# Sums for the activations' operands, and the third norm's factor and bias, moved from GpSimd to VectorE

## Chip, cores and metric

The kernel runs on one core of a Trainium2 chip. The metric is device time in microseconds (us), the median of three runs. The engines are TensorE (PE in the rows; PEld is its weight load), VectorE (DVE), ScalarE (ACT), GpSimd (POOL) and SyncE (SP), which issues the DMAs. Each works off its own queue in order.

## Reference

One decoder block, batch 1, 1024 tokens, width 1024, in float32: a SwiGLU layer (inner width 2816), a token mixer (short convolution beside a diagonal state space), a second SwiGLU layer and a gated embedding, each followed by a layer norm. Cut to what matters here:

```python
def layer_norm(x, g, b):
    xc = x - mean(x)
    return xc * rsqrt(mean(xc * xc) + LN_EPS) * g + b

x = layer_norm(ALPHA * x + 0.5 * swiglu(x, ffn1_w_in, ffn1_w_out), ln1_g, ln1_b)
mix = token_mixer(x, mix_w_in, ...)
x = layer_norm(ALPHA * x + mix, ln2_g, ln2_b)
x = layer_norm(ALPHA * x + 0.5 * swiglu(x, ffn2_w_in, ffn2_w_out), ln3_g, ln3_b)
e = (p @ ple_w_in) * sigmoid(x @ ple_w_gate)
x = layer_norm(ALPHA * x + e, ln4_g, ln4_b)
```

## The kernel before

**Products.** Every float32 operand is split into a rounded high part and a remainder (`split`, lines 175 and 176: ScalarE casts the high part, VectorE, or GpSimd where the code says so, subtracts it to get the low part), and a product is three passes of matmuls: high by high, high by low, low by high. Weights come as tiles `Ws` of 128x512 and are split into `Wh` and `Wl`.

**Seven products in place of eight.** The input layers (`w_in` of both SwiGLU layers and of the mixer) multiply 2x2 blocks by a Strassen-Winograd scheme. A pair of weight rows (`Pair`) needs seven operands of the activations: 11 and 21 are blocks as they are, 22 also, and t1, t2, t3 and t4 are sums of blocks: t1 = 12 - 11, t2 = 22 - t1, t3 = 22 - 12, t4 = 21 - t2. The same sums of weights (`Pair.rest`, lines 79, 84, 88, 96 and 102) run on GpSimd, and the change does not touch them.

**Where the activations' sums are made.** In three places. At the kernel's start `first_operands.later` (lines 426 to 437) makes them from `x` in two column groups j of 128x1024: j = 0 on VectorE, j = 1 on GpSimd. After the first and after the second layer norm `winograd_sink` (lines 365 to 373) gets two token tiles at a time, transposed by TensorE (line 281) and given factor and bias by ScalarE (line 283, `features`). For token pairs i = 2 and 3 it makes the four sums for each j: j = 0 on GpSimd, j = 1 on VectorE. Low parts of 11 and 21 (`x11l`, `x21l`) are mostly on GpSimd and stay there. While this goes on, TensorE works on the products by 11 and 21 of the first five pairs (`EARLY`, tiles `early`) and then needs t1, t2, t3, 22 and t4.

**The last stage** (from line 1229). For each of eight token tiles s: `apply(acc2[s])` gives factor and bias of the third layer norm to the residual stream (`affine`, lines 315 and 316: first half of the columns on VectorE, second half on GpSimd, each a multiply and an add of 128x512). Then, for each half of the columns, 24 matmuls make the gate into a `pm` bank (line 1243; there are six) and 6 matmuls the embedding into a `pt` bank (line 1248; there are two). ScalarE makes `sg`, the sigmoid (line 1251, a buffer of tag `T`; there are six, and the four rows `gb` of factor and bias are of that tag too), VectorE multiplies embedding and sigmoid (line 1252, which frees both banks' data) and adds the product to the residual stream (line 1253). The fourth layer norm follows (`moments`, lines 248 to 255, and lines 1257 and 1258), and a DMA writes the result.

**The order** of each engine's queue is set at build time by a scheduler that goes by dependences and its own estimate of times. `issue_after` adds an edge that keeps what is traced inside it, on the same engine, behind a given instruction.

Of the kernel before, what the change touches and what calls it, by code (L numbers as in the profile page):

```python
# [12 lines left out]
ALU = mybir.AluOpType  # L13
# [92 lines left out]
class Block:  # L106
# [194 lines left out]
    def affine(self, g, b, tag):  # L301

        if tag == "A8":
            both = self.t("A8", [P, 2, D], name="gb")
            gb = [both[:, v, 512 * h:512 * h + 512] for v in range(2) for h in range(2)]
        else:
            gb = [self.t(tag, [P, 512], name="gb") for _ in range(4)]
        for i, part in enumerate(gb):
            self.nc.sync.dma_start(part, (g, b)[i // 2][i % 2 * 512:i % 2 * 512 + 512].partition_broadcast(P))

        def apply(t):
            for h in range(2):
                sl = slice(h * 512, (h + 1) * 512)
                eng = (self.nc.vector, self.nc.gpsimd)[h]
                eng.tensor_tensor(t[:, sl], t[:, sl], gb[h], ALU.mult)
                eng.tensor_tensor(t[:, sl], t[:, sl], gb[2 + h], ALU.add)  # L316
        return apply


# [20 lines left out]
    def winograd_sink(self, xs, gb):  # L340

        kept = []
        gps = self.nc.gpsimd

        def put(name, y, i, j, eng=None):
            cols, ks = slice((i % 2) * 256, (i % 2 + 1) * 256), slice(2 * j, 2 * j + 2)
            hi, lo = xs[name]
            self.split(y, hi[:, ks, cols], lo[:, ks, cols], eng)

        def sink(i, pair):  # L350
            if i < 2:
                kept.append([self.t("H", [P, 4, 256], name="y") for _ in range(2)])
                for kh in range(2):
                    for j in range(2):
                        y = kept[i][kh][:, 2 * j:2 * j + 2]
                        self.features(pair, gb, 4 * kh + 2 * j, y)
                        put(("11", "21")[kh], y, i, j, None if (kh, j) == (0, 1) else gps)
                return
            for j in range(2):
                b11, b21 = (kept[i - 2][kh][:, 2 * j:2 * j + 2] for kh in range(2))  # L360
                b12, b22 = self.t("T", [P, 2, 256], name="b12"), self.t("T", [P, 2, 256], name="b22")
                t1 = self.t("T", [P, 2, 256], name="t1")
                self.features(pair, gb, 2 * j, b12)
                eng = (gps, self.nc.vector)[j]
                eng.tensor_tensor(t1, b12, b11, ALU.subtract)
                put("t1", t1, i, j)
                self.features(pair, gb, 4 + 2 * j, b22)
                put("22", b22, i, j)
                eng.tensor_tensor(b12, b22, b12, ALU.subtract)
                put("t3", b12, i, j)  # L370
                eng.tensor_tensor(t1, b22, t1, ALU.subtract)
                put("t2", t1, i, j)
                eng.tensor_tensor(t1, b21, t1, ALU.subtract)
                put("t4", t1, i, j)
        return sink
# [4 lines left out]
    def first_operands(self, xT, w_in):  # L380

        nc = self.nc
        xs = self.new_xs()
        self.open_region("init")
        p, w = {}, {}
        early = FIRST[:EARLY]

        def weight(f, kh):
            w[f, kh] = self.stage(w_in[f][kh])

        def piece(n, j):
            kh, th = int(n[0]) - 1, int(n[1]) - 1
            p[n, j] = self.r("xp", [P, 2, 512], 8)
            return xT[:, kh, th, 2 * j:2 * j + 2, :]

        def put(n, j, y, ks=slice(0, 2)):
            hi, lo = xs[n]
            k0 = slice(2 * j + ks.start, 2 * j + ks.stop)
            self.split(y[:, ks], hi[:, k0], lo[:, k0])

        weight(early[0], 0)
        for j in range(2):
            src = piece("11", j)
            for k in range(2):
                ks = slice(k, k + 1)
                nc.sync.dma_start(p["11", j][:, ks], src[:, ks])
                put("11", j, p["11", j], ks)
            weight(early[1 + j], 0)
        for f in early[3:]:
            weight(f, 0)  # L410
        for j in range(2):
            src = piece("21", j)
            nc.sync.dma_start(p["21", j], src)
            put("21", j, p["21", j])
        for n in ("12", "22"):
            for f in (early[:2] if n == "12" else early[2:]):
                weight(f, 1)
            for j in range(2):
                src = piece(n, j)
                nc.sync.dma_start(p[n, j], src)  # L420

        def later():
            tt = [self.t("H", [P, 2, 512], name="t1") for _ in range(2)]
            eng = (nc.vector, nc.gpsimd)
            for j in range(2):
                eng[j].tensor_tensor(tt[j], p["12", j], p["11", j], ALU.subtract)
                put("t1", j, tt[j])
            for j in range(2):
                eng[j].tensor_tensor(tt[j], p["22", j], tt[j], ALU.subtract)
                put("t2", j, tt[j])  # L430
            for j in range(2):
                eng[j].tensor_tensor(p["12", j], p["22", j], p["12", j], ALU.subtract)
                put("t3", j, p["12", j])
            for j in range(2):
                put("22", j, p["22", j])
            for j in range(2):
                eng[j].tensor_tensor(tt[j], p["21", j], tt[j], ALU.subtract)
                put("t4", j, tt[j])
        return xs, w, later

# [708 lines left out]
    def run(self, a, out):  # L1149
        nc = self.nc  # L1150
# [41 lines left out]
        acc2, last = self.mixer(state["x"], a, acc)  # L1192
# [19 lines left out]
        apply = self.affine(a["ln3_g"], a["ln3_b"], "T")  # L1212
# [11 lines left out]
        for v in ("ln4_g", "ln4_b"):  # L1224
            for h in range(2):
                tl = self.t("Ws", [P, 512], name="gb4")
                nc.sync.dma_start(tl, a[v][h * 512:(h + 1) * 512].partition_broadcast(P))
                gb4.append(tl)
        for s in range(NT):
            cols = slice((s % 4) * P, (s % 4 + 1) * P)  # L1230
            if s % 2 == 0:
                pp = self.split_w(self.stage(a["pT"][:, s // 2]))
            apply(acc2[s])
            pcol = lambda k: slice((2 * (s % 2) + k) * P, (2 * (s % 2) + k + 1) * P)
            cuts = HALVES if s < NT - 1 else (slice(0, 512), slice(512, 768), slice(768, D))
            for sl in cuts:
                dh, n = sl.start // 512, sl.stop - sl.start
                col = slice(sl.start - 512 * dh, sl.stop - 512 * dh)
                pg = self.pm()[:, :n]
                for k in range(NK):  # L1240
                    xx = self.op(xb[k // 4][s // 4])
                    for i, (p, q) in enumerate(((0, 0), (0, 1), (1, 0))):
                        nc.tensor.matmul(pg, xx[p](k % 4)[:, cols], wg[dh][k][q][:, col],  # L1243
                                         start=(k == 0 and i == 0), stop=(k == NK - 1 and i == 2))
                pe = self.pt()[:, :n]
                for k in range(2):
                    for i, (p, q) in enumerate(((0, 0), (0, 1), (1, 0))):
                        nc.tensor.matmul(pe, pp[p][:, pcol(k)], wp[q][:, k, sl], start=(k == 0 and i == 0),  # L1248
                                         stop=(k == 1 and i == 2))
                sg = self.t("T", [P, 512], name="sg")[:, :n]  # L1250
                nc.scalar.activation(sg, pg, AF.Sigmoid)
                nc.vector.tensor_tensor(sg, pe, sg, ALU.mult)
                nc.vector.scalar_tensor_tensor(acc2[s][:, sl], sg, 1.0 / ALPHA, acc2[s][:, sl], ALU.mult, ALU.add)
            mean, y, _ = self.moments(acc2[s], cuts)
            for dh, sl in enumerate(HALVES):
                t = acc2[s][:, sl]
                nc.vector.scalar_tensor_tensor(t, t, mean, gb4[dh], ALU.subtract, ALU.mult)
                nc.vector.scalar_tensor_tensor(t, t, y, gb4[2 + dh], ALU.mult, ALU.add)
                nc.sync.dma_start(out[:, s, sl], t)
# [62 lines left out]
```

## Time and profile before

| what | value |
|---|---|
| median of three runs | 2084.79 us (2083.38 to 2086.32) |
| the profiled execution's own time | 2086.58 us |
| its span, first to last instruction | 2084.8 us |
| mean granted TensorE clock | 0.991 |
| busy: PE, DVE, ACT, POOL | 96%, 80%, 39%, 41% of the span |

The profile is one execution. A row of its timeline says when an instruction (or a run of equal ones, xN) started, how long it took, and in brackets how long its engine had been idle before it and what ended that. The clock is in shares of 2.4 GHz: 1.00 is 2.4 GHz, 0.50 is 1.2 GHz.

### The profile page before, as it was taken

What the parts mean: (1) busy time and instruction counts of PE and PEld (TensorE: products, weight loads), DVE (VectorE), ACT (ScalarE), POOL (GpSimd) and SP (SyncE); (2) the same over time, 40 slices, a digit from 0 to 9 for tenths busy, and PEclk for the clock granted to TensorE, in tenths of its full rate; (3) what the DMA queues carried; (4) which work ended last, traced back from release to release, by engine and by line L of the source; (5) the groups of instructions that cost most, each with busy time, mean ns of one, the idle gap of its engine ahead of it and who ended that gap; (6) DMA issues with size and microseconds to landing.
All of it is one profiled execution on the core that took longest, in us unless ns stands there. A gap on an engine that the chain in (4) does not pass through costs nothing.

```text
span 2084.8 us, 26465 instructions
## 1 busy us (share of the span) xinstructions
PE 2001.7 (96%) x9030; PEld 1633.4 (78%) x9030; DVE 1668.0 (80%) x2560; ACT 813.7 (39%) x1422; POOL 846.4 (41%) x562
## 2 busy tenths in 40 slices
PE   7999999999999899999999999999999999999988
PEld 5887778776788777887878888788888876788867
DVE  7789888879998976767644679877667789998897
ACT  5333343445342545343533415533333345342520
POOL 3644444454313454333201372654444444313360
PEclk9999999999999999999999999999999999999999
DMA  4433343556540264333382410243323246431111
GB/s 170 127 117 96 122 141 126 179 186 223 164 141 25 106 187 148 100 122 114 133 299 80 151 53 17 83 149 117 101 87 126 91 166 217 162 128 69 54 45 69
DMA packets 153238, 260.24 MB, mean 125 GB/s; under 512 B 16144, under 2 KB 61200, under 8 KB 153104
## 3 DMA queue, kind: packets, MB, share of 16 engines
q1 hardware_dynamic: 153104, 258.56, 37.6%
q8 instruction: 71, 1.16, 0.2%
q14 instruction: 63, 0.52, 0.1%
HBM read 189.85 MB, written 68.65 MB: 124 GB/s over the span
## 4 chain that ended last, share of the span: by engine, by line
PE 67%; DVE 21%; issue 5%; DMA 2%; ACT 2%; POOL 2%; SPq 0%; DVEq 0%; POOLq 0%; ACTq 0%
PE pm L198 42%; PE pm L615 11%; PE pm L209 5%; PE pm L229 5%; DVE Wl L176 4%; PE pm L1243 2%; DVE wt L176 2%; DVE w L176 1%; DVE acc L622 1%; DVE ln L254 1%; PE pt L1248 1%; DVE ln L248 1%; DVE ln L255 1%; DVE acc L316 1%; DVE acc L234 1%
## 5 line engine op out<-in xcount | busy, mean ns | idle before, releaser
L175 ACT CAST Wh<-Ws 128x512 fp32r<-128x512 f32 x268 | 166.6, 622 | 346.5 <-PE pm L198 277.5
L176 DVE TENSOR_TENSOR Wl<-Ws,Wh 128x512 fp32r<-128x512 f32 x268 | 212.8, 799 | 109.1 <-ACT Wh L175 108.7
L175 ACT CAST Wh<-s 128x512 fp32r<-128x512 f32 x240 | 149.2, 622 | 379.2 <-PE pm L198 139.3
L176 DVE TENSOR_TENSOR Wl<-s,Wh 128x512 fp32r<-128x512 f32 x240 | 213.5, 890 | 25.8 <-ACT Wh L175 25.7
L615 PE MATMUL pm<-wt,Wh 128*128 128x512 f32 x640 | 188.0, 392 | 2.5 <-DVE acc L622 2.5
L84 POOL TENSOR_TENSOR s<-s,Ws 128x512 f32<-128x512 f32 x60 | 90.2, 1503 | 203.6 <-DVE Wl L176 193.3
L102 POOL TENSOR_TENSOR u<-u,p 128x512 f32<-128x512 f32 x60 | 96.1, 1602 | 144.3 <-DVE u L92 93.2
L615 PE MATMUL pm<-w,Wh 128*128 128x512 f32 x480 | 141.4, 392 | 6.1 <-ACT Wh L175 5.5
L622 DVE SCALAR_TENSOR_TENSOR acc<-pm,acc 128x512 f32<-128x512 f32 x200 | 132.7, 682 | 15.5 <-PE pm L615 14.8
L615 PEld LDWEIGHTS pm<-wt,Wh 128*128 128x128 f32 x640 | 119.7, 188 | 30.2 <-DVE acc L622 3.3
L79 POOL TENSOR_TENSOR s<-Ws 128x512 f32<-128x512 f32 x60 | 82.5, 1374 | 133.8 <-DVE Wl L176 102.0
L96 POOL TENSOR_TENSOR s<-Ws,s 128x512 f32<-128x512 f32 x60 | 92.3, 1538 | 108.8 <-DVE Wl L176 107.4
L615 PE MATMUL pm<-wt,Wl 128*128 128x512 f32 x320 | 113.8, 394 | 3.9 <-DVE Wl L176 3.6
L615 PEld LDWEIGHTS pm<-w,Wh 128*128 128x128 f32 x480 | 90.0, 189 | 26.8 <-ACT Wh L175 7.1
L198 PE MATMUL pm<-x11h,Wh 128*128 128x512 f32 (+1 forms) x264 | 99.1, 384 | 5.0 <-ACT x11h L175 5.0
L198 PE MATMUL pm<-x11h,Wl 128*128 128x512 f32 (+1 forms) x264 | 99.3, 379 | 3.1 <-DVE Wl L176 3.1
L198 PE MATMUL pm<-x11l,Wh 128*128 128x512 f32 (+1 forms) x264 | 99.6, 380 | 1.9 <-DVE x11l L176 1.3
L198 PE MATMUL pm<-xt1h,Wl 128*128 128x512 f32 x240 | 95.3, 397 | 5.3 <-DVE Wl L176 5.3
L198 PE MATMUL pm<-x21h,Wl 128*128 128x512 f32 x240 | 95.1, 396 | 5.5 <-DVE Wl L176 5.5
L198 PE MATMUL pm<-xt2h,Wl 128*128 128x512 f32 x240 | 94.8, 395 | 4.2 <-DVE Wl L176 4.1
L198 PE MATMUL pm<-xt4h,Wl 128*128 128x512 f32 x240 | 94.1, 392 | 4.6 <-DVE Wl L176 4.6
L198 PE MATMUL pm<-xt1l,Wh 128*128 128x512 f32 x240 | 94.4, 393 | 2.1 <-DVE xt1l L176 2.1
(355 smaller groups left out, 5615.7 us busy)
## 6 DMA issues: line engine op xcount, KB each, us to landing
Ws<-in_ffn_w_in SPq DMA_DIRECT2D x196, 256.0 KB, 2.7
Ws<-in_ffn_w_out SPq DMA_DIRECT2D x88, 256.0 KB, 3.1
Ws<-in_w_mix SPq DMA_DIRECT2D x74, 256.0 KB, 2.7
s<-h_s SPq DMA_DIRECT2D x60, 256.0 KB, 3.0
h<-a SPq DMA_DIRECT2D x58, 256.0 KB, 2.3
ha<-h SPq DMA_DIRECT2D x20, 512.0 KB, 4.1
hb<-h SPq DMA_DIRECT2D x20, 512.0 KB, 4.6
h_s<-u SPq DMA_DIRECT2D x20, 256.0 KB, 2.6
```

Source lines behind the costliest of these rows:

```text
L79: gps.tensor_tensor(s, a21, a22, ALU.add)
L84: gps.tensor_tensor(s, s, a11, ALU.subtract)
L96: gps.tensor_tensor(s, a12, s, ALU.subtract)
L102: gps.tensor_tensor(u3, u3, p5, ALU.add)
L175: self.nc.scalar.copy(hi, src)
L176: (lo_eng or self.nc.vector).tensor_tensor(lo, src, hi.bitcast(F32), ALU.subtract)
L198: self.nc.tensor.matmul(ps[:, tok], w[a][:, sl], x[b](k)[:, tok], start=(start and k == 0 and i == 0), stop=(k == nk - 1 and i == 2), skip ...
L209: self.nc.tensor.matmul(ps[h], w[a][:, sl], x(h)[b](k), start=(k == 0 and i == 0), stop=(k == 3 and i == 2))
L229: nc.tensor.matmul(ps, a[:, s * P:(s + 1) * P], b[:, cols], start=(j == 0 and i == 0), stop=(j == n - 1 and i == 2))
L615: nc.tensor.matmul(ps[i], hh[p][:, cols], w[n][:, j, q], start=(start and j == 0 and k == 0), stop=(j == 1 and k == 2), skip_group_check=n ...
L622: vec.scalar_tensor_tensor(t, ps[i], scale, t, ALU.mult, ALU.add)
L1243: nc.tensor.matmul(pg, xx[p](k % 4)[:, cols], wg[dh][k][q][:, col], start=(k == 0 and i == 0), stop=(k == NK - 1 and i == 2))
```

## The change

All sums that make operands of the activations go to VectorE (lines 365 to 373 and 426 to 437), and so do both halves of the third norm's factor and bias. Before the first token tile nothing else changes there. From the second on, the four operations of `apply` stand, by `issue_after`, behind the last product of embedding and sigmoid of the token tile before. No operation is added or left out; 36 are moved from GpSimd to VectorE (4 of 128x1024, 32 of 128x512, namely 8 in each call of the sink for the two norms and 16 in the last stage).

```diff
@@ affine @@
         def apply(t):
+            vec = self.nc.vector
             for h in range(2):
                 sl = slice(h * 512, (h + 1) * 512)
-                eng = (self.nc.vector, self.nc.gpsimd)[h]
-                eng.tensor_tensor(t[:, sl], t[:, sl], gb[h], ALU.mult)
-                eng.tensor_tensor(t[:, sl], t[:, sl], gb[2 + h], ALU.add)
+                vec.tensor_tensor(t[:, sl], t[:, sl], gb[h], ALU.mult)
+                vec.tensor_tensor(t[:, sl], t[:, sl], gb[2 + h], ALU.add)
         return apply
@@ winograd_sink @@
                 self.features(pair, gb, 2 * j, b12)
-                eng = (gps, self.nc.vector)[j]
+                eng = self.nc.vector
                 eng.tensor_tensor(t1, b12, b11, ALU.subtract)
@@ first_operands @@
         def later():
             tt = [self.t("H", [P, 2, 512], name="t1") for _ in range(2)]
-            eng = (nc.vector, nc.gpsimd)
+            vec = nc.vector
             for j in range(2):
-                eng[j].tensor_tensor(tt[j], p["12", j], p["11", j], ALU.subtract)
+                vec.tensor_tensor(tt[j], p["12", j], p["11", j], ALU.subtract)
                 put("t1", j, tt[j])
...
@@ run @@
+        last = None
         for s in range(NT):
             cols = slice((s % 4) * P, (s % 4 + 1) * P)
             if s % 2 == 0:
                 pp = self.split_w(self.stage(a["pT"][:, s // 2]))
-            apply(acc2[s])
+
+            with self.tc.issue_after(last.ins) if last else ExitStack():
+                apply(acc2[s])
...
-                nc.vector.tensor_tensor(sg, pe, sg, ALU.mult)
+                last = nc.vector.tensor_tensor(sg, pe, sg, ALU.mult)
```

In the new kernel the lines of the last stage stand three further down: 1243, 1248, 1251, 1252, 1253, 1257 and 1258 are now 1246, 1251, 1254, 1255, 1256, 1260 and 1261.

VectorE's queue at the start of the last stage, before (`acc` is the residual stream, `gb` a row of factor or bias, `ln` the statistics of the norm):

```order
L176 TENSOR_TENSOR Wl<-Ws,Wh 128x512 x3
L315 TENSOR_TENSOR acc<-acc,gb 128x512 x8
L316 TENSOR_TENSOR acc<-acc,gb 128x512 x3
L1252 TENSOR_TENSOR sg<-pt,sg 128x512
L316 TENSOR_TENSOR acc<-acc,gb 128x512 x2
L1252 TENSOR_TENSOR sg<-pt,sg 128x512
L316 TENSOR_TENSOR acc<-acc,gb 128x512 x3
L1253 SCALAR_TENSOR_TENSOR acc<-sg,acc 128x512
```

The same place of the same queue now:

```order
L176 TENSOR_TENSOR Wl<-Ws,Wh 128x512 x3
L315 TENSOR_TENSOR acc<-acc,gb 128x512 x2
L316 TENSOR_TENSOR acc<-acc,gb 128x512
L1255 TENSOR_TENSOR sg<-pt,sg 128x512
L316 TENSOR_TENSOR acc<-acc,gb 128x512
L1256 SCALAR_TENSOR_TENSOR acc<-sg,acc 128x512
L1255 TENSOR_TENSOR sg<-pt,sg 128x512
L315 TENSOR_TENSOR acc<-acc,gb 128x512 x2
L248 BN_STATS ln<-acc 128x6
L1256 SCALAR_TENSOR_TENSOR acc<-sg,acc 128x512
L316 TENSOR_TENSOR acc<-acc,gb 128x512 x2
```

Eleven operations of factor and bias stood ahead of the first product of embedding and sigmoid; now three do, and the two halves of a token tile and its successor's four operations take turns.

GpSimd's queue after the first norm, before (`t` and `b` are the sums' tiles, `y` the block 11 or 21, `s` and `Ws` the weights' sums):

```order
L176 TENSOR_TENSOR x21l<-y,x21h 128x2x256
L365 TENSOR_TENSOR t_6185<-b_6183,y 128x512
L176 TENSOR_TENSOR x21l<-y,x21h 128x2x256
L369 TENSOR_TENSOR b_6183<-b_6184,b_6183 128x512
L371 TENSOR_TENSOR t_6185<-b_6184,t_6185 128x512
L79 TENSOR_TENSOR s<-Ws 128x512
L88 TENSOR_TENSOR Ws<-Ws 128x512
L365 TENSOR_TENSOR t_6305<-b_6303,y 128x512
L373 TENSOR_TENSOR t_6185<-y,t_6185 128x512
L369 TENSOR_TENSOR b_6303<-b_6304,b_6303 128x512
L371 TENSOR_TENSOR t_6305<-b_6304,t_6305 128x512
L84 TENSOR_TENSOR s<-s,Ws 128x512
```

and now:

```order
L176 TENSOR_TENSOR x21l<-y,x21h 128x2x256 x2
L79 TENSOR_TENSOR s<-Ws 128x512
L88 TENSOR_TENSOR Ws<-Ws 128x512
L84 TENSOR_TENSOR s<-s,Ws 128x512
L96 TENSOR_TENSOR s<-Ws,s 128x512
```

Only the low parts and the weights' sums are left there; the place after the second norm reads alike. On VectorE the moved sums stand among the splits in their own order, each ahead of the low part that needs it.

## Rows read from the trace of the kernel before

**Rows 1.** Busy time by stretch: length, PE, PEld, DVE, ACT, POOL, PEclk, DMA share, GB/s.
```profile
28.00:48.00 20.00, 13.18 (x46) 9.25 (x45) 20.00 (x14) 11.42 (x15) 11.86 (x6) 0.89 0.15 45
711.00:748.00 37.00, 31.48 (x144) 23.62 (x145) 33.88 (x48) 29.01 (x56) 23.94 (x12) 1.00 0.45 136
1290.00:1330.00 40.00, 33.55 (x145) 25.39 (x145) 36.27 (x50) 29.41 (x56) 26.05 (x14) 0.96 0.18 53
1986.00:2020.00 34.00, 24.00 (x88) 18.57 (x87) 33.87 (x28) 6.72 (x11) 29.89 (x18) 0.85 0.06 17
```
**Rows 2.** PE's waits, 28 to 48 us: us in total, times, longest.
```profile
PE pm L198 <- DVE Wl L176: 6.8, 4, 3.2
```
**Rows 3.** PE's waits, 711 to 748 us.
```profile
PE pm L198 <- DVE Wl L176: 3.5, 4, 1.4
...
PE pm L198 <- ACT Wh L175: 0.7, 2, 0.4
```
**Rows 4.** PE's waits, 1290 to 1330 us.
```profile
PE pm L198 <- DVE Wl L176: 3.8, 3, 2.3
PE pm L198 <- DVE xt1l L176: 1.8, 1, 1.8
```
**Rows 5.** PE's timeline, last stage: start, us, instruction [idle before, releaser].
```profile
1997.74 0.39 PE L1243 MATMUL pm<-wgh,xl 128*128 128x512 f32 x1
2005.27 1.22 PE L1248 MATMUL pt<-wp,Wh 128*128 128x512 f32 x2 [7.14 <-DVE sg L1252]
...
2009.27 0.73 PE L1248 MATMUL pt<-wp,Wh 128*128 128x512 f32 x2
...
2013.72 0.39 PE L1243 MATMUL pm<-wgl,xh 128*128 128x512 f32 x1
2016.14 1.07 PE L1248 MATMUL pt<-wp,Wh 128*128 128x512 f32 x2 [2.03 <-DVE sg L1252]
...
2019.57 0.47 PE L1243 MATMUL pm<-wgl,xh 128*128 128x512 f32 x1
```
**Rows 6.** The chain that ended last, in the last stage: start, us, what.
```profile
2041.39 5.44 PE pm L1243 x24
2046.83 1.36 PE pt L1248 x6
```
**Rows 7.** DVE's timeline, last stage.
```profile
1986.06 13.54 DVE L315 TENSOR_TENSOR acc<-acc,gb 128x512 f32<-128x512 f32 x8 [1.19 <-DMA gb<-in_ln_g]
...
2004.53 0.68 DVE L1252 TENSOR_TENSOR sg<-pt,sg 128x512 f32<-128x512 f32 x1
```
**Rows 8.** Groups of DVE, 2020 to 2060 us: count, busy us, mean ns, idle before.
```profile
L1257 DVE SCALAR_TENSOR_TENSOR acc<-acc,ln,gb 128x512 f32<-128x512 f32 x12 | 8.7, 744 | 0.0
...
L254 DVE SCALAR_TENSOR_TENSOR ln<-ln 128x1 f32<-128x1 f32 x18 | 3.6, 208 | 0.0
```
**Rows 9.** DVE's timeline at the kernel's start.
```profile
16.95 3.49 DVE L426 TENSOR_TENSOR t<-xp 128x1024 f32<-128x1024 f32 x1
...
24.65 1.22 DVE L429 TENSOR_TENSOR t<-xp,t 128x1024 f32<-128x1024 f32 x1
25.78 3.47 DVE L432 TENSOR_TENSOR xp<-xp 128x1024 f32<-128x1024 f32 x1
```
**Rows 10.** DVE's timeline after the first norm.
```profile
716.68 1.28 DVE L176 TENSOR_TENSOR Wl<-Ws,Wh 128x512 fp32r<-128x512 f32 x2
717.88 0.68 DVE L369 TENSOR_TENSOR b<-b,b 128x512 f32<-128x512 f32 x1
...
725.52 1.57 DVE L176 TENSOR_TENSOR Wl<-Ws,Wh 128x512 fp32r<-128x512 f32 x1 [2.74 <-ACT Wh L175]
...
731.03 1.76 DVE L176 TENSOR_TENSOR Wl<-Ws,Wh 128x512 fp32r<-128x512 f32 x1
```
**Rows 11.** POOL's timeline after the first norm.
```profile
716.84 7.09 POOL L371 TENSOR_TENSOR t<-b,t 128x512 f32<-128x512 f32 x1 [3.84 <-DVE xt1l L176]
```
**Rows 12.** ACT's waits, 711 to 748 us.
```profile
ACT b L283 <- POOL t L371: 2.7, 1, 2.7
```

More of the change, by code (lines that the diff above doesn't have):

```diff
@@ L423, in later @@
             tt = [self.t("H", [P, 2, 512], name="t1") for _ in range(2)]
-            eng = (nc.vector, nc.gpsimd)
+            vec = nc.vector
             for j in range(2):
-                eng[j].tensor_tensor(tt[j], p["12", j], p["11", j], ALU.subtract)
+                vec.tensor_tensor(tt[j], p["12", j], p["11", j], ALU.subtract)
                 put("t1", j, tt[j])
             for j in range(2):
-                eng[j].tensor_tensor(tt[j], p["22", j], tt[j], ALU.subtract)
+                vec.tensor_tensor(tt[j], p["22", j], tt[j], ALU.subtract)
                 put("t2", j, tt[j])
             for j in range(2):
-                eng[j].tensor_tensor(p["12", j], p["22", j], p["12", j], ALU.subtract)
+                vec.tensor_tensor(p["12", j], p["22", j], p["12", j], ALU.subtract)
                 put("t3", j, p["12", j])
@@ L436, in later @@
             for j in range(2):
-                eng[j].tensor_tensor(tt[j], p["21", j], tt[j], ALU.subtract)
+                vec.tensor_tensor(tt[j], p["21", j], tt[j], ALU.subtract)
                 put("t4", j, tt[j])
```

## Prediction

> **What bounds the kernel now.** First the table of busy shares: TensorE works in 96% of the span, so a gain can only come from stretches in which it waits, and from the time in which it runs at its lower clock. The busy time by stretch, read beside the timeline, leaves four that hold the lines of the change [rows 1]: the kernel's start, the places after the first and the second norm, and the last stage. In each of them VectorE is the engine that is full (20.00 of 20.00 us, 33.88 of 37.00, 36.27 of 40.00, 33.87 of 34.00), GpSimd works for more than half of the time, and TensorE lacks 6.8, 5.5, 6.5 and 10 us. Then the waits of TensorE in those stretches, to see for whom it waits: 6.8 us for VectorE's low parts at the start [rows 2], 3.5 us after the first norm and 0.7 us for ScalarE's casts [rows 3], 3.8 and 1.8 us after the second [rows 4]. In the last stage it stands for 7.14 and 2.03 us until VectorE has multiplied embedding and sigmoid, since that empties one of the two embedding banks [rows 5]. So VectorE ends the waits everywhere, and the question is what the change does to VectorE's queue there.
>
> **The last stage.** An undisturbed half token tile takes TensorE 5.44 us for 24 gate matmuls and 1.36 us for six embedding matmuls, that is 0.227 us each [rows 6]. The last gate matmul before the first stop starts at 1997.74, so the next was due at 1997.97; it starts at 2005.27, 7.30 us late. The nine matmuls from there to 2009.27 take 4.00 us, where nine of 0.227 take 2.04: 1.96 us lost. The second stop: due at 2013.95, starts at 2016.14, 2.19 us; the eight matmuls up to 2019.57 take 3.43 in place of 1.81 us, 1.62 lost [rows 5]. Those slow matmuls stand right behind the idle times, at 0.44 us each, which is the lower level of the clock, 1.2 GHz; the granted clock of the whole stretch is 0.85 [rows 1]. Sum of what the two stops cost: 7.30 + 1.96 + 2.19 + 1.62 = **13.1 us**.
>
> Both stops come from the queue: the first product of embedding and sigmoid starts at 2004.53, behind eleven operations of factor and bias. The first eight of these took 13.54 us, 1.69 each [rows 7], while GpSimd ran its own half beside them. An operation of the same size with two operands in SBUF starts 0.60 us after its predecessor where GpSimd does not work: two splits from 716.68, and the next operation at 717.88 [rows 10]. So an operation next to GpSimd holds VectorE for 1.09 us more.
>
> Now the queue reads two multiplies, one add, then the first product. The first two still meet GpSimd's last two low parts, so I leave them at 1.69: 1986.06 + 3.38 + 0.60 + 0.60 = 1990.6 for the first product's end, and with one add, one sum and one more product 1992.4 for the second's. In TensorE's new queue the third embedding stands 20 matmuls earlier, 4.5 us, thus due at 1993.4: still behind both. The first stop goes. Afterwards each token tile costs VectorE 14 large operations (four of factor and bias, two products, two sums, two statistics, four of the fourth norm) and 11 of one column. At their longest, 0.744 and 0.208 us [rows 8], that is 10.4 + 2.3 = 12.7 us, against TensorE's 2 x 6.80 = 13.6 us. VectorE stays just ahead, so no later stop has to follow, and all 13.1 us are taken. What is left behind the last matmul is the same as before.
>
> What else comes late: the rows of factor and bias hold four of the six `T` buffers until the last tile now, so the sigmoid has two. It gets one back when the sum two halves earlier is done. That is hidden as long as VectorE is not a full half tile behind.
>
> **The start.** Four sums of 128x1024 join VectorE, four leave GpSimd. Alone such an operation costs 1.13 us (24.65 to 25.78), next to GpSimd 3.49 and 3.47 us [rows 9], so it is held for about 2.3 us. Four VectorE operations are held that way between 16.95 and 44.4 us, one for each moved sum: 4 x 2.3 = 9.2 us go, 4 x 1.14 = 4.6 come, VectorE's queue gets 4.6 us shorter. TensorE waits there 6.8 us for that queue [rows 2], so I take **4.6 us**. The bounds: 0, if the weights' sums on GpSimd move up into the free time and hold VectorE instead; 6.8, if all waits go.
>
> **After the first norm.** Eight sums of 128x512 come, 8 x 0.60 = 4.8 us. Beside the eight that leave GpSimd, six VectorE operations are held by up to 1.09 us; the split at 731.03 with its 1.76 us is one of them [rows 10]: 6 x 1.09 = 6.5 us go. Net 1.7 us shorter. The second part is an idle time in a full queue: VectorE waits 2.74 us at 725.52 for ScalarE's cast [rows 10], ScalarE 2.7 us for GpSimd's sum of line 371 [rows 12], and that one took 7.09 us [rows 11], since VectorE ran one operation behind the other. On VectorE it takes 0.60. So the queue gets 1.7 + 2.7 = 4.4 us shorter. TensorE's waits for its results there are 3.5 + 0.7 us [rows 3]; I take **4.0 us**, bounds 0 and 4.2.
>
> Of those 7.09 us the Trainium skill (SBUF — State Buffer, section Who interferes with whom) would expect less: it tells of a lock of the shared read port in which the second to start is blocked until the first has finished, thus for one operation of VectorE and not for a whole run of them. By that rule GpSimd's sum would have ended some 5 us earlier, the 2.7 us would have another cause and stay, and the two norms would give 1.7 us each and the whole 21.1 us. The row shows the longer hold, so I keep the 2.7.
>
> **After the second norm.** The same code and the same count: eight sums come, six held operations go, and the same idle time of VectorE is seen; 4.4 us of queue, against 3.8 + 1.8 us of TensorE's waits [rows 4]. I take **4.4 us**, bounds 0 and 5.6.
>
> Nothing else moves: the other queues change order only in these four places, and between them TensorE is full, so what is won in one place is carried to the end.
>
> **Sum.** 4.6 + 4.0 + 4.4 + 13.1 = 26.1 us. The profiled execution took 2086.6 us (span 2084.8 and 1.8 around it), so 2060.5 for a profiled one; the median of the runs is 1.8 us below the profiled one, so **2059 us**.
>
> **Rivals.**
> A, the forecast: 2054 to 2063 us, since the three smaller terms have their bounds.
> B, the sums give nothing: the weights' sums of GpSimd fill the time that the others leave and hold VectorE as before, and what is relieved is paid back by what is added. Only the last stage gains: 2084.8 - 13.1 = 2072 us. For it: the four lines of weights' sums remain in GpSimd's queue at all three places. Against it: they wait for other things there, and the two idle times of 2.7 us go in any case.
> C, the slower side: VectorE's 1.7 us are its own in these full stretches and not GpSimd's doing. Then each moved operation costs and nothing is given back: 4.6 + 4.8 + 4.8 = 14.2 us; and in the last stage a tile costs VectorE 4 x 1.69 + 10 x 0.744 + 2.3 = 16.5 us against 13.6, eight tiles 23 us more, from which the 13.1 are taken: 10 us. 2109 us. It decides from about half: with a share h of the 1.09 us staying, the outcome runs from -26 to +24 us, zero at h = 0.5. Against it: large operations at 0.744 at most as soon as GpSimd is quiet [rows 8], in the same stage.
> The Trainium skill (Perfetto Trace Analysis, section Optimizing Scalar/DVE Operations) speaks for C: a saturated VectorE may be relieved by giving work to ScalarE or even GpSimd, and here a full VectorE gets more. The same sentence goes on that a shared read port may make it useless between these two; by the first half 2109, by the second A.
> D, two `T` buffers are too few, or VectorE falls behind once more: two stops such as the second one return, 2 x 3.8 us: 2066 us. For it: 12.7 against 13.6 is little room.
> E, all waits go and the lower clock behind them too (0.89 and 0.96 granted [rows 1], 1.4 and 1.3 us): 6.8 + 4.2 + 5.6 + 13.1 + 2.7 = 32.4, 2052 us.
> That the order would not be as the change says is excluded by the queue's listing above.
>
> **How the numbers follow.** A 0.60, B 0.13, C 0.04, D 0.13, E 0.08, and 0.02 that the gains are lost in something that I do not see and nothing changes. Range: A, D and E, that is 2051 to 2070 us, 0.81. About 0.2% (4 us) is what a measurement of this kernel can tell from no change: faster 0.94, same 0.02, slower 0.04.
>
> **What would show it.** In the profile after: no wait of TensorE for the products of the last stage and a granted clock of 1.00 there, operations of factor and bias at about 0.7 us; the first t1 product after the second norm some 4 us earlier against the stretch's start; no wait of ScalarE for line 371, no idle time of VectorE there. It is wrong if VectorE's low parts beside the weights' sums stay at 1.7 us as often as before (B), if splits without GpSimd beside them are slow (C), or if TensorE waits for the products between 2005 and 2030 us (D).

## The result, and the profile after

The changed kernel takes 2061.05 us (median of 4 runs, 2060.84 to 2062.38) against 2085.03 us for the kernel before on the same chip: ratio 0.9887, 95% interval 0.987 to 0.9904, 24.0 us less. On another chip it gave 2062.6 us, ratio 0.9893 (0.9877 to 0.991). The profiled execution took 2061.11 us, its span is 2059.1. The first part of its page:

```profile
span 2059.1 us, 26438 instructions
...
PE 1993.1 (97%) x9030; PEld 1630.6 (79%) x9030; DVE 1649.6 (80%) x2596; ACT 812.7 (39%) x1422; POOL 793.8 (39%) x526
```

The four stretches of [rows 1], moved 5, 4, 12 and 12 us ahead so that each holds about the same work (columns as there):

```profile
23.00:43.00 20.00, 16.44 (x66) 12.48 (x64) 20.00 (x18) 13.33 (x18) 7.03 (x3) 0.94 0.22 73
707.00:744.00 37.00, 34.85 (x164) 27.14 (x163) 33.27 (x56) 30.45 (x59) 20.09 (x6) 1.00 0.60 192
1278.00:1318.00 40.00, 35.61 (x167) 29.07 (x166) 37.84 (x67) 31.14 (x60) 21.17 (x8) 0.91 0.20 54
1974.00:2008.00 34.00, 33.17 (x147) 27.15 (x146) 34.00 (x69) 7.71 (x12) 2.31 (x2) 1.00 0.08 29
```

TensorE's work rises from 24.00 to 33.17 of 34 us in the last stage, and its granted clock there from 0.85 to 1.00. VectorE is as full as before, but it does 69 instructions in that stretch where it did 28. In the other three stretches TensorE gains 3.3, 3.4 and 2.1 us of work; after the second norm 4.4 us of waits remain, and the clock is no better (0.96 before, 0.91 now).

The last stage in VectorE's timeline, which answers to [rows 7]:

```profile
1973.69 3.17 DVE L315 TENSOR_TENSOR acc<-acc,gb 128x512 f32<-128x512 f32 x2 [1.36 <-DMA gb<-in_ln_g]
1976.79 0.68 DVE L316 TENSOR_TENSOR acc<-acc,gb 128x512 f32<-128x512 f32 x1
1977.39 0.68 DVE L1255 TENSOR_TENSOR sg<-pt,sg 128x512 f32<-128x512 f32 x1
1977.99 0.68 DVE L316 TENSOR_TENSOR acc<-acc,gb 128x512 f32<-128x512 f32 x1
```

Two multiplies are still held by GpSimd's last low parts (3.17 us for the pair), then every operation starts 0.60 us behind the one ahead. The first product starts 3.70 us behind the first multiply; before it was 18.47. TensorE waits for no product; its only wait in this stage, 0.8 us for the first sigmoid, is in the kernel before too. ScalarE does wait, in the stretch 1974 to 2008, for the `T` buffers that rival D spoke of, and nobody waits for the sigmoids that come of it:

```profile
ACT sg L1254 <- DVE acc L1256: 14.6, 6, 4.4
```

**Where the time went, by place.** The start of one and the same matmul is read in both timelines of TensorE. For the kernel's start, for instance, the first xt1 product starts at 42.43 us before and at 35.69 now, 6.74 earlier; the first product with block 21 (22.87 and 21.36) was 1.51 earlier already (TensorE left the lower clock sooner, ahead of the first moved sum), which leaves 5.2 us for the place. In the same way: first transposes of the first norm 683.94 and 679.91, first matmul of the mixer behind its operands 772.57 and 765.02, third transpose of the second norm 1271.65 and 1261.71, xt1 product of the fourth pair behind the five early ones 1450.33 and 1437.33, third gate matmul of high by high (`wgh`, `xh`) 1945.24 and 1932.28, last one of these 2074.54 and 2048.64. For all profiled kernels, us won against the kernel before (the rest is what the span won besides, nearly all of it between these places, where the code is the same):

| kernel | start | after first norm | after second norm | last stage | rest | median, us against before |
|---|---|---|---|---|---|---|
| the change | 5.2 | 3.5 | 3.1 | 13.0 | +1.0 | -24.0 |
| after_again | 5.2 | 3.7 | 2.8 | 13.1 | -0.7 | -22.3 |
| sums_part | 5.2 | 3.5 | 2.9 | -0.1 | +1.7 | -10.8 |
| last_part | 0.1 | 0.1 | 0.2 | 14.2 | -3.4 | -11.5 |
| order_alone | 0.8 | 0.1 | -0.5 | 9.3 | +0.7 | -7.9 |
| engine_alone | -0.5 | -0.2 | 0.0 | 13.0 | -2.5 | -9.9 |
| no_order | 5.2 | 3.5 | 2.7 | 13.1 | -2.7 | -20.6 |
| gps_load | 5.2 | 3.5 | 3.1 | -5.7 | -2.9 | -2.1 |
| gps_write | 5.2 | 3.6 | 2.9 | 13.2 | -0.1 | -23.1 |
| weights1 | 6.0 | 6.2 | 6.6 | 13.2 | -1.3 | -31.4 |
| weights1_again | 6.0 | 6.2 | 6.5 | 13.2 | +0.8 | -30.6 |
| weights2 | 6.0 | 4.6 | 7.4 | 13.2 | -0.2 | -28.0 |

Where the code of a place is the same, it repeats to some tenths of a microsecond, at the worst 0.8 us (the start in order_alone); the one larger difference, the 14.2 of last_part, is explained below. The rest doesn't repeat, it differs between executions by up to 5 us. Some of it lies right behind the first place: between 42 and 55 us the lead still changes, by -0.4 us in the change, by -2.2 in gps_write, and by +0.8 in engine_alone, which has no change there. Part of it is the clock in unchanged code; two such stretches, first of the kernel before, then of the changed one (columns as above):

```profile
455.00:485.00 30.00, 26.74 (x115) 20.91 (x114) 28.89 (x37) 17.16 (x32) 15.67 (x11) 1.00 0.94 330
1066.00:1086.00 20.00, 17.09 (x70) 13.68 (x69) 5.90 (x10) 3.36 (x6) 0.00 (x0) 0.91 0.89 332
```

```profile
455.00:485.00 30.00, 25.93 (x104) 20.72 (x103) 27.91 (x37) 16.34 (x29) 13.30 (x9) 0.89 0.89 313
1066.00:1086.00 20.00, 17.86 (x78) 14.27 (x77) 8.35 (x14) 4.58 (x8) 0.00 (x0) 1.00 0.88 328
```

In the first stretch the changed kernel loses 2.4 us, most of it at a granted clock of 0.89 behind a wait of TensorE that was 2.76 us and is 4.07; in the second it is the kernel before that stands at 0.91, and the changed one wins 2.3, about half of it by the clock. Neither stretch holds a line of the change. So a term of 1 us can be read from a place here, but not from two medians.

### The profile page after: what moved, and what is told of

The parts are those of the page before. It is cut to its first block, busy times and chain, and to the rows that moved or that the text cites. A ratio compares the mean times of both kernels' runs of the same rounds, so it can differ in the third digit from the quotient of the medians.

```text
span 2059.1 us, 26438 instructions
## 1 busy us (share of the span) xinstructions
PE 1993.1 (97%) x9030; PEld 1630.6 (79%) x9030; DVE 1649.6 (80%) x2596; ACT 812.7 (39%) x1422; POOL 793.8 (39%) x526
## 4 chain that ended last, share of the span: by engine, by line
PE 69%; DVE 18%; issue 5%; DMA 3%; POOL 3%; ACT 1%; SPq 0%; DVEq 0%; POOLq 0%; ACTq 0%
PE pm L198 42%; PE pm L615 12%; PE pm L209 6%; PE pm L229 5%; DVE Wl L176 3%; PE pm L1246 3%; DVE wt L176 2%; DVE acc L622 1%; DVE w L176 1%; POOL s L79 1%; PE pt L1251 1%; DVE ln L254 1%; DVE ln L248 1%; DMA Ws<-in_ffn_w_in 1%; POOL s L84 1%
## 5 line engine op out<-in xcount | busy, mean ns | idle before, releaser
L176 DVE TENSOR_TENSOR Wl<-Ws,Wh 128x512 fp32r<-128x512 f32 x268 | 202.7, 761 | 103.8 <-ACT Wh L175 103.3
L79 POOL TENSOR_TENSOR s<-Ws 128x512 f32<-128x512 f32 x60 | 98.7, 1645 | 178.3 <-DVE Wl L176 112.4
L615 PEld LDWEIGHTS pm<-wt,Wh 128*128 128x128 f32 x640 | 120.3, 189 | 31.4 <-DVE acc L622 3.5
L198 PE MATMUL pm<-xt2h,Wh 128*128 128x512 f32 x240 | 94.8, 395 | 4.2 <-ACT Wh L175 4.1
L198 PE MATMUL pm<-x22h,Wl 128*128 128x512 f32 x240 | 94.7, 395 | 0.7 <-DVE Wl L176 0.6
```

Of the source, the lines that this page charges most:

```text
L79: gps.tensor_tensor(s, a21, a22, ALU.add)
L176: (lo_eng or self.nc.vector).tensor_tensor(lo, src, hi.bitcast(F32), ALU.subtract)
L198: self.nc.tensor.matmul(ps[:, tok], w[a][:, sl], x[b](k)[:, tok], start=(start and k == 0 and i == 0), stop=(k == nk - 1 and i == 2), skip ...
L615: nc.tensor.matmul(ps[i], hh[p][:, cols], w[n][:, j, q], start=(start and j == 0 and k == 0), stop=(j == 1 and k == 2), skip_group_check=n ...
```

## The experiments

### The two halves of the change apart

The theory: an operation of GpSimd holds the VectorE operation beside it, and the last stage's stops come from the eleven held operations ahead of the first product. Rival B: the sums give nothing. Rival C: VectorE's 1.7 us are its own. last_part is the change without the sums:

```diff
-                eng = (self.nc.vector, self.nc.gpsimd)[h]
-                eng.tensor_tensor(t[:, sl], t[:, sl], gb[h], ALU.mult)
...
+                vec.tensor_tensor(t[:, sl], t[:, sl], gb[h], ALU.mult)
...
+            with self.tc.issue_after(last.ins) if last else ExitStack():
+                apply(acc2[s])
...
```

> Only the last stage changed (factor and bias on VectorE, in the order of need); all sums stay split between VectorE and GpSimd. My theory, that an operation of GpSimd holds the VectorE operation beside it and that the last stage's two stops come from the eleven operations ahead of the first product: 13.1 us below the kernel before, 2072 us, and no wait of TensorE for the products. Rival B (the sums give nothing): 2061 us, the whole gain. Rival C (VectorE's 1.7 us are its own): 10 us above before, 2095 us.

Measured: 2074.31 us, ratio 0.9943 (0.9928 to 0.9957), 11.5 us below before and 2.3 above what was expected; 14.2 us in the last stage by place, with 3.4 lost in the rest, and no wait for a product. sums_part is the other half:

```diff
-                eng = (gps, self.nc.vector)[j]
+                eng = self.nc.vector
...
-            eng = (nc.vector, nc.gpsimd)
+            vec = nc.vector
...
-                eng[j].tensor_tensor(tt[j], p["12", j], p["11", j], ALU.subtract)
+                vec.tensor_tensor(tt[j], p["12", j], p["11", j], ALU.subtract)
...
```

> Only the sums moved to VectorE (kernel's start, after the first and the second norm); the last stage as before. My theory: 12 to 13 us below before, 2072 us, with the last stage's stops of 7.3 and 2.2 us unchanged. Rival B: 2085 us, no change, since the weights' sums on GpSimd fill the free time. Rival C: 14 us above before, 2099 us.

Measured: 2075.01 us, ratio 0.9949 (0.9932 to 0.9965), 10.8 us below and 3 above what was expected; the last stage is as before, with TensorE's two stops in it:

```profile
1991.80 1.22 PE L1248 MATMUL pt<-wp,Wh 128*128 128x512 f32 x2 [7.11 <-DVE sg L1252]
2002.66 0.92 PE L1248 MATMUL pt<-wp,Wh 128*128 128x512 f32 x2 [1.89 <-DVE sg L1252]
```

The halves add up (22.3 us against 22.3 and 24.0 for both). Rival B is out, since the sums alone give 11.6 us at their three places. Rival C is out: it wanted both above before.

### Order or engine

In the last stage the change does two things, and each was put into the kernel before alone. order_alone keeps half of factor and bias on GpSimd:

```diff
+            with self.tc.issue_after(last.ins) if last else ExitStack():
                 apply(acc2[s])
...
-                nc.vector.tensor_tensor(sg, pe, sg, ALU.mult)
+                last = nc.vector.tensor_tensor(sg, pe, sg, ALU.mult)
```

> Only the order of need in the last stage, on the kernel before: factor and bias of a token tile are queued behind the last product of the tile before, but the second half of each still runs on GpSimd. If the order is what counts (rival): the first product stands behind one multiply and one add, the first stop goes, 13 us below before, 2072 us. If GpSimd's operations beside VectorE count as well (my theory): the first stop goes, but two GpSimd operations for each token tile hold two of VectorE's by 1.09 us, 12.7 - 1.2 + 2.2 = 13.7 us for a tile against TensorE's 13.6, so later waits return and the gain is 6 to 12 us, 2073 to 2079 us.

Measured: 2077.91 us, ratio 0.996 (0.9946 to 0.9974), 7.9 us below; 9.3 us in the last stage. One wait of TensorE for a product is left, 2.8 us. Within the range, but not by the course that I had written: GpSimd doesn't do two operations for each token tile, it does all sixteen at once, as POOL's timeline shows, and the wait that is left ends in those 26 us, at 2013.50.

```profile
1988.13 13.19 POOL L315 TENSOR_TENSOR acc<-acc,gb 128x512 f32<-128x512 f32 x8
2001.29 12.69 POOL L316 TENSOR_TENSOR acc<-acc,gb 128x512 f32<-128x512 f32 x8
```

engine_alone is the first diff above without the order, its two lines of `issue_after` and `apply`:

> Only the engine in the last stage, on the kernel before: all factors and biases on VectorE, in the order the scheduler makes without the tie (in VectorE's queue sixteen of them stand ahead of the first product, eleven more behind the second). If the engine is what counts: the sixteen take 16 x 0.60 + 2.2 = 11.8 us where eleven took 18.5, so the first product comes some 6 us earlier and most of the 13.1 us are won: 2073 to 2076 us. If the order counts more: the eleven operations behind the second product take 6.6 us and make a new stop at the fourth embedding, and less than 6 us are won: 2079 us or above. Rival C: 27 operations at 1.7 us, above before.

Measured: 2075.87 us, ratio 0.9948 (0.9933 to 0.9963), 9.9 us below; 13.0 us in the last stage, all of it. VectorE's timeline there:

```profile
1988.77 11.04 DVE L315 TENSOR_TENSOR acc<-acc,gb 128x512 f32<-128x512 f32 x15 [1.39 <-DMA gb<-in_ln_g]
1999.73 0.68 DVE L316 TENSOR_TENSOR acc<-acc,gb 128x512 f32<-128x512 f32 x1
2000.34 0.68 DVE L1252 TENSOR_TENSOR sg<-pt,sg 128x512 f32<-128x512 f32 x1
...
2001.54 0.68 DVE L1252 TENSOR_TENSOR sg<-pt,sg 128x512 f32<-128x512 f32 x1
2002.14 6.70 DVE L316 TENSOR_TENSOR acc<-acc,gb 128x512 f32<-128x512 f32 x11
```

Sixteen operations ahead of the first product, and it still starts 11.57 us behind the first multiply where it was 18.47. The eleven behind the second product take 6.70 us; TensorE's queue has its third embedding later in this kernel, at 2003.69, and no stop follows. no_order is the whole change without the order:

```diff
-            with self.tc.issue_after(last.ins) if last else ExitStack():
-                apply(acc2[s])
+            apply(acc2[s])
```

> The changed kernel without the order of need: factor and bias and all sums on VectorE, the last stage in the scheduler's own order, sixteen of the operations ahead of the first product. If the engine does nearly all of it, as the kernel with the engine alone showed (13.0 us in its last stage against 14.2 with the order): 2061 to 2063 us. If the order matters once more is won upstream: 2065 us or above.

Measured: 2064.56 us, between the two ranges; the ratio, 0.9902 (0.9888 to 0.9917), has an interval that overlaps that of the change (0.987 to 0.9904). By place it wins 13.1 us in the last stage, as the change does; the 3.5 us between the medians lie in the rest. last_part, with the order, has 1.2 us more than engine_alone in its last stage, but 1.0 of that lies ahead of the first factor: TensorE waits there for line 265 of the third norm, 0.8 us in the kernel before, 0.9 in engine_alone and 1.0 in the change, and not in last_part. So the engine alone does it. The order alone gets 9.3 of the 13 us, and beside the engine it adds nothing that these runs can tell.

### Is it GpSimd that holds VectorE?

In the last stage of the changed kernel GpSimd has nothing to do. gps_load gives it 25 sums that nobody needs:

```diff
+        self.gb3 = gb
...
+            if s == 0:
+                idle = self.t("E", [P, 512], name="idle")
+                nc.gpsimd.tensor_tensor(idle, self.gb3[0], self.gb3[2], ALU.add)
+            for _ in range(3):
+                nc.gpsimd.tensor_tensor(idle, idle, self.gb3[2], ALU.add)
```

> The changed kernel, with 25 extra sums of 128x512 on GpSimd in the last stage, where GpSimd has nothing else to do; they read the rows of factor and bias and a tile of their own, nobody waits for them, and the other engines' queues are the same, instruction for instruction. My theory (an operation of GpSimd holds the one of VectorE beside it for 1.09 us): 25 x 1.09 = 27 us more in VectorE's queue, of which its room of 0.9 us for a token tile takes up to 7; VectorE's large operations at 1.7 us again beside them, waits of TensorE for the products, 2066 to 2088 us, about 2080. Rival C (the 1.7 us are VectorE's own in a full stretch): no change, 2061 us. If GpSimd only waits while VectorE is busy: 2061 us as well, with GpSimd's operations at 5 us and more.

Measured: 2083.02 us, ratio 0.9989 (0.998 to 0.9999): nearly the whole gain is gone, with the same instructions in the same order on every engine but GpSimd. GpSimd's row, TensorE's waits (us in total, times, longest) and VectorE's groups (count, busy us, mean ns) while it lasts; in this kernel and the next, lines 315 and 316 of factor and bias are 317 and 318, and those from 1246 on stand seven further down:

```profile
1981.35 40.46 POOL L1243 TENSOR_TENSOR idle<-idle,gb 128x512 f32<-128x512 f32 x24
```

```profile
PE pt L1258 <- DVE sg L1262: 11.8, 3, 4.7
```

```profile
L318 DVE TENSOR_TENSOR acc<-acc,gb 128x512 f32<-128x512 f32 x12 | 15.0, 1265 | 0.0
L317 DVE TENSOR_TENSOR acc<-acc,gb 128x512 f32<-128x512 f32 x11 | 12.3, 1137 | 0.1
L1263 DVE SCALAR_TENSOR_TENSOR acc<-sg,acc 128x512 f32<-128x512 f32 x10 | 10.6, 1058 | 0.0
L1267 DVE SCALAR_TENSOR_TENSOR acc<-acc,ln,gb 128x512 f32<-128x512 f32 x6 | 7.3, 1228 | 0.0
L1262 DVE TENSOR_TENSOR sg<-pt,sg 128x512 f32<-128x512 f32 x10 | 6.8, 677 | 0.0
L248 DVE BATCH_NORM_STATS2 ln<-acc 128x6 f32<-128x512 f32 x8 | 5.3, 679 | 0.0
```

The operations with two large operands in SBUF (factor and bias, L317 and L318; the sum L1263; the fourth norm L1267) are held to 1.06 to 1.27 us on average; in the changed kernel the same groups have 0.69 and 0.75. Over the first four groups that is 18.4 us of VectorE. The product of line 1262, one of whose operands is in PSUM, and the statistics, which read one tile, keep their 0.68 us. TensorE pays 11.8 us of waits, and the granted clock is 0.87 from 1979 to 2030. By place the last stage loses 18.7 us against the change. gps_write asks what of GpSimd's work it is:

```diff
-                nc.gpsimd.tensor_tensor(idle, idle, self.gb3[2], ALU.add)
+                nc.gpsimd.memset(idle, 0.0)
```

> The changed kernel with the same 25 extra operations on GpSimd in the last stage, but 24 of them only write (a fill with zero) where the run with the sums read two tiles. That run lost 22 us, and in it VectorE's operations with two operands in SBUF were held (1.06 to 1.27 us on average), those with one operand in PSUM or with a single operand not (0.68). If it is the reading of SBUF that two operations share: nothing is held, 2061 to 2064 us. If any operation of GpSimd beside VectorE holds it: 2075 to 2088 us as with the sums.

Measured: 2061.8 us, ratio 0.9891 (0.9876 to 0.9906), like the change. POOL's row, and VectorE's rows at its beginning:

```profile
1978.69 13.98 POOL L1243 MEMSET idle<- 128x512 f32 x24
```

```profile
1977.41 1.77 DVE L318 TENSOR_TENSOR acc<-acc,gb 128x512 f32<-128x512 f32 x1
...
1981.50 1.28 DVE L317 TENSOR_TENSOR acc<-acc,gb 128x512 f32<-128x512 f32 x2
1982.70 0.68 DVE L248 BATCH_NORM_STATS2 ln<-acc 128x6 f32<-128x512 f32 x1
1983.31 0.67 DVE L1263 SCALAR_TENSOR_TENSOR acc<-sg,acc 128x512 f32<-128x512 f32 x1
1983.90 1.28 DVE L318 TENSOR_TENSOR acc<-acc,gb 128x512 f32<-128x512 f32 x2
```

The operation at 1977.41 meets the one sum that was left (1976.90 to 1978.63) and is held; beside the fills the same operations run at 0.60 us each. The fills end after 14 us where the sums lasted 40, so the dose in time is smaller; in those 14 us nothing is held at all. So it is not writing that holds VectorE; what the sums have and the fills lack is the reading of SBUF. A fill is also shorter, 0.58 us against 1.69, and no run takes the two differences apart. The Trainium skill (SBUF — State Buffer, section Who interferes with whom) says just this: VectorE with two inputs in SBUF contends with a GpSimd operation that reads SBUF and not with one that only writes, and with at most one input there, outside its two-port modes, it doesn't contend. The rows of gps_load and gps_write agree.

### The stall that moved

After the second norm the changed kernel has a wait of TensorE that took 0.65 us in the kernel before:

```profile
1308.54 0.79 PE L198 MATMUL pm<-xt2h,Wh 128*128 128x512 f32 x1 [3.93 <-ACT Wh L175]
```

ScalarE's cast of those weights waited 4.11 us for a weights' sum of GpSimd, line 84; after the first norm a cast waits likewise for line 79 (ScalarE's waits, 707 to 744 and 1278 to 1318 us):

```profile
ACT Wh L175 <- POOL s L79: 3.0, 1, 3.0
...
ACT Wh L175 <- POOL s L84: 4.1, 1, 4.1
```

POOL's timeline of the changed kernel after the first norm and after the second, and VectorE's at the end of the first of these rows:

```profile
717.82 11.30 POOL L79 TENSOR_TENSOR s<-Ws 128x512 f32<-128x512 f32 x1 [12.29 <-DVE Wl L176]
729.20 1.30 POOL L88 TENSOR_TENSOR Ws<-Ws 128x512 f32<-128x512 f32 x1
...
1288.84 7.79 POOL L79 TENSOR_TENSOR s<-Ws 128x512 f32<-128x512 f32 x1 [9.32 <-DMA Ws<-in_ffn_w_in]
...
1302.58 5.26 POOL L84 TENSOR_TENSOR s<-s,Ws 128x512 f32<-128x512 f32 x1 [4.24 <-DVE Wl L176]
```

```profile
727.30 0.68 DVE L176 TENSOR_TENSOR xt4l<-t,xt4h 128x512 fp32r<-128x512 f32 x1
729.81 1.24 DVE L176 TENSOR_TENSOR Wl<-s,Wh 128x512 fp32r<-128x512 f32 x1 [1.83 <-ACT Wh L175]
```

An operation that takes 1.3 to 1.6 us takes 5.26, 7.79 and 11.30 where VectorE runs one operation with two SBUF operands behind the other. The longest begins at 717.82, sixteen operations of VectorE begin and end beside it, and it ends at 729.12, 1.1 us after the last of them: it came through when VectorE had nothing left, since VectorE in turn waited for it, by way of the cast. The 5.26 us ended in the same way. The 7.79 us did not: VectorE went on at 1295.46 and was held itself, and what let GpSimd in there stays open. The 7.09 us of line 371 [rows 11] were of this kind; now the weights' sums have them. weights1 is the change with the sums of the first pair behind each set of operands on VectorE too, five operations at each of three places:

```diff
...
-        nc, gps, vec = blk.nc, blk.nc.gpsimd, blk.nc.vector
+        nc, vec = blk.nc, blk.nc.vector
+        gps = vec if self.near else blk.nc.gpsimd
...
+            p.near = i < 1
```

> The changed kernel, and the weights' sums of the first pair behind each new set of operands (five operations at three places) on VectorE too. After the second norm the changed kernel still stands 3.9 us for one of them, a sum on GpSimd that took 5.26 us beside a dense run of VectorE and 1.6 alone. If that is the same hold as the one of line 371: this wait goes, two to four held operations of VectorE (1.09 us each) go at each place, 3.0 us of sums come at each: 2054 to 2059 us. If VectorE is simply too full there: 3 x 3.0 us more, 2064 to 2070 us.

> The changed kernel with the first pair's five weights' sums at each of the three places on VectorE, once more: 7 us below the changed kernel, 2054 us, with 6 us after the first norm, 6.5 us after the second and 6 us at the start against the kernel before. If the 7 us were only a lucky run: 2058 to 2061 us.

Measured: 2053.76 us, ratio 0.985 (0.9833 to 0.9866), and again 2054.23, 0.9853 (0.9838 to 0.9867), against 0.9893 (0.9877 to 0.991) for the change beside the second of them: the first pair's sums are worth 8.4 us more by these two medians, some 7 by place. By place 6.2 us after the first norm (3.5 with the change), 6.5 after the second (3.1), 6.0 at the start (5.2). The stretches of the second execution, columns as above:

```profile
707.00:744.00 37.00, 35.45 (x166) 28.57 (x166) 36.39 (x60) 29.12 (x56) 4.20 (x3) 1.00 0.59 193
...
1278.00:1318.00 40.00, 38.50 (x170) 29.57 (x171) 39.21 (x64) 30.86 (x59) 8.04 (x4) 1.00 0.24 73
```

GpSimd is nearly idle there, VectorE is fuller than ever (36.39 of 37, 39.21 of 40), and TensorE works more. weights2 does the same for two pairs (`i < 2`):

> As the kernel before this one, for the first two pairs: ten operations at each of the three places on VectorE. If held operations are what VectorE loses there: another 2 to 4 us less than with the first pair alone, 2051 to 2057 us. If each place has its end with the first pair, and the second pair's sums only add 3.0 us to a full queue: 2056 to 2066 us, above the kernel with the first pair alone.

Measured: 2057.2 us, ratio 0.987 (0.9855 to 0.9884). The second pair gives 0.8 us more after the second norm and takes 1.6 after the first, so it is no better than the first pair alone; the interval overlaps that of weights1, and whether it is worse stays open. weights1 has the lowest median here.

Confirmation of the change itself:

> The changed kernel once more, beside the next one on the same chip: 24 us below the kernel before, 2061 us. In its profile the terms by place should repeat: about 5 us at the start (to the first t1 product), 3.5 us after the first norm, 3 us after the second, 13 us in the last stage, with 1 to 3 us of difference in stretches that the change doesn't touch.

Measured: 2062.6 us, 22.3 below before in place of 24, and the places as expected, 5.2, 3.7, 2.8 and 13.1 us.

## Why the prediction was right, step by step

The forecast was 2059 us with a range of 2051 to 2070; 2061 came out. The four terms were 4.6, 4.0, 4.4 and 13.1 us and measured 5.2, 3.5, 3.1 and 13.0. That is 24.8 us in place of 26.1; the rest gave 1.0 back, and the 1.8 us by which the profiled execution before lay above its median did not come again.

**The last stage** was right in its sum, 13.0 us, and in the mechanism: the stops and the lower clock behind them go together. What I gave too much weight is the order. The argument went by the count of operations ahead of the first product, eleven then and three now; engine_alone has sixteen ahead and wins the same. What counts is the time that they take in all: sixteen in 11.57 us make no stop, eleven in 18.47 make two. 12.7 us of VectorE against 13.6 of TensorE for a token tile held: VectorE is full up to 2014.8, then has work for 13.41 and 13.01 us in the next two stretches of 13.6, and TensorE waits for no product. The row that the 0.60 us were read from was not free of GpSimd, as I had it: line 371 was under way from 716.84 [rows 11] and was itself the one that was held. The figure stands all the same, since in the changed kernel's last stage, with GpSimd idle, the steps are 0.60 us too.

**The start** had the four held operations right. Beside the two of [rows 9] they are the split at 29.18 and one of the two at 39.88; over 0.68, 1.21 and 1.22 us alone these four lose 8.9 us, where I had 9.2. VectorE's timeline before has two more held operations, at 31.93 and 34.17, but those stand beside the weights' sums of GpSimd, not beside a moved one (VectorE's rows, then GpSimd's):

```profile
29.18 2.83 DVE L176 TENSOR_TENSOR Wl<-Ws,Wh 128x512 fp32r<-128x512 f32 x1
31.93 2.31 DVE L176 TENSOR_TENSOR xt2l<-t,xt2h 128x1024 fp32r<-128x1024 f32 x1
34.17 1.78 DVE L176 TENSOR_TENSOR Wl<-Ws,Wh 128x512 fp32r<-128x512 f32 x1
...
39.88 4.58 DVE L176 TENSOR_TENSOR x22l<-xp,x22h 128x1024 fp32r<-128x1024 f32 x2
```

```profile
31.43 1.73 POOL L79 TENSOR_TENSOR s<-Ws 128x512 f32<-128x512 f32 x1
33.24 2.16 POOL L88 TENSOR_TENSOR Ws<-Ws 128x512 f32<-128x512 f32 x1
```

In the changed kernel the weights' sums moved up into the free time, as the lower bound said they might, and hold two operations as they did before, 2.2 us then and now:

```profile
26.35 2.31 DVE L432 TENSOR_TENSOR xp<-xp 128x1024 f32<-128x1024 f32 x1
28.58 1.78 DVE L176 TENSOR_TENSOR Wl<-Ws,Wh 128x512 fp32r<-128x512 f32 x1
```

What was mis-counted is what comes: only three of the four moved sums stand ahead of the xt1 weights, 3.4 us and not 4.6. With 0.8 us of idle time gone that is 8.9 + 0.8 - 3.4 = 6.3 us of VectorE's queue, of which TensorE shows 5.2. A wait of 3.26 us for VectorE stays there, right behind the first xt1 product.

**After the two norms** the step that failed is "ScalarE waits for GpSimd's sum of line 371 ... on VectorE it takes 0.60", from which I let the 2.7 us of VectorE's idle time vanish. Line 371 takes 0.69 us now and nobody waits for it. But the stall went to the next operation that GpSimd still has: after the first norm ScalarE waits 3.0 us for line 79, and VectorE is idle for 1.8 us behind that cast (and for 1.6 behind line 283, which waited for TensorE); after the second the wait reaches TensorE with 3.93. So 3.5 and 3.1 us came in place of 4.0 and 4.4, and of the signs that I had named, the first t1 product after the second norm came 2.6 us earlier and not 4. Half of rival B is in this: the weights' sums do take the place of those that left, by being held and by holding. Eight and nine of VectorE's operations of 128x512 took 1.5 us or more in these two stretches before, one and four of them beside weights' sums alone; three and five still do, all of them beside weights' sums. Two of the five:

```profile
1297.11 1.77 DVE L176 TENSOR_TENSOR xt1l<-t,xt1h 128x512 fp32r<-128x512 f32 x1
...
1309.73 1.78 DVE L371 TENSOR_TENSOR t<-b,t 128x512 f32<-128x512 f32 x1
```

That the weights' sums are the cause, weights1 shows, which takes the first pair's away and gets 6.2 and 6.5. How much of it is their being held and how much their holding, no run tells.

The Trainium skill's rule on the lock (the same section), by which the second to start is blocked until the first has finished, was weighed against 7.09 us in the prediction. The rows after differ from it more clearly still: 11.30 us for an operation on GpSimd, in which VectorE began and ended sixteen. Where GpSimd's operations stand one behind the other (gps_load, 1.69 us each) it is VectorE that is held, for one operation at a time. Here the measurement decides.

**"Between them TensorE is full, so what is won in one place is carried to the end"** held only on the whole: between the places from -3.4 to +1.7 us come and go, in part with the clock. That it was +1.0 in the profiled execution is luck.

Rival D's reason was real (14.6 us of ScalarE's waits for `T` buffers) and cost nothing, since TensorE had gate matmuls to do meanwhile. Rival E's lower clock at the start and after the second norm did not go: 0.94 and 0.91 are granted there now.

## What to carry to other kernels

Before work is given to GpSimd to relieve a full VectorE, count what it costs there: where both read two operands from SBUF, a sum of 128x512 on GpSimd held VectorE for at least 0.74 us on average here (18.4 us for 25 in gps_load), and VectorE would have done it in 0.60. And if VectorE runs densely, an operation of GpSimd that somebody waits for may take 5 to 11 us in place of 1.5; when one of these is moved away, look for the next one that GpSimd still has in the same stretch, since the stall goes there. VectorE's operations that read PSUM, or only one tile, stood beside GpSimd here at no cost (0.68 us each).

## What the runs showed of the hardware

- A sum on GpSimd beside dense work of VectorE is not only slowed but starved: 5.26, 7.79 and 11.30 us, against 1.3 to 1.6 otherwise. I had expected that of line 371 alone. GpSimd's sums one behind the other (1.69 us each) hold VectorE instead.
- The hold depends on what both do: 25 sums on GpSimd cost 18.7 us in the last stage and 22 by the medians, one sum and 24 fills nothing.
- Whether TensorE's clock falls behind a wait in unchanged code differs from execution to execution (0.89 and 1.00 in one stretch). It is part of what makes two profiled executions differ by up to 5 us outside the places, while the places themselves repeat to some tenths of a microsecond.
